# A two-layer conv-FFN backbone: another order of products in the up phase, paired accumulators, and earlier loads in the down phase

## The chip, the cores and the metric

The kernel runs on one core of a Trainium2 chip. The metric is the time of one execution in microseconds (us); runs are told by their median. The engines are TensorE (PE, with its weight loads PEld), VectorE (DVE), ScalarE (ACT), GpSimd (POOL) and SyncE (SP), on which most transfers are asked for. Each works through its own queue in order.

## What is computed

Two layers over 1024 latent tokens and 256 context tokens of width 1024. Each layer is a mixer followed by a gated FFN with a convolution of three taps along the tokens. Only the FFN with its norms, and the output projection ahead of it, matter here:

```python
def conv_ffn(h, w_up, conv_w, conv_b, w_down):
    u = dwconv(h @ w_up, conv_w, conv_b)
    return (jax.nn.silu(u[..., :D_FF]) * u[..., D_FF:]) @ w_down
...
        x = x + mods_x[2] * out_x
        x = x + mods_x[5] * conv_ffn(modulate(x, mods_x[3], mods_x[4]), ffn_w_up[layer], ffn_conv_w[layer],
                                     ffn_conv_b[layer], ffn_w_down[layer])
```

D_FF is 2816, that is 22 tiles of 128 features, each with a gate and an up half. In layer 0 the context tokens go through the same FFN; layer 1 needs the latent tokens alone.

## The kernel before, in words

Numbers are fp32. A product of full accuracy is made of three matmuls: every operand is split into a high part (a copy on ACT, L64) and a low part (a subtraction on DVE, L65), and high x high, low x high and high x low are added up in PSUM (L253 to L255). So each weight tile that comes in as wraw becomes wh (ACT) and wl (DVE) before PE can use it.

An FFN has three stages. `emit_out` makes the output projection in chunks of tokens (512, 512, and 256 of context); each result is drained from PSUM by DVE into the residual xr (L1322), and a norm follows each chunk: squares on ACT (L145), their sum on DVE (L147), a sum over partitions on PE (L151), an inverse square root by Newton steps on DVE (L71 to L81).

`emit_up` walks over the 22 features f. The first is made densely. For the others the 1024 latent tokens and the 1024 inputs are taken as 2x2 blocks b00, b01, b10, b11, and seven block products of 12 matmuls with 512 columns give what eight would (a scheme of the Strassen kind): t1, t2, t4 are sums of blocks made once per layer, and the weights' sums are made for each feature on POOL (ws, L363, L364, L367, L368) from the raw weights a (gate) and b (up) and then split into wsh and wsl. In layer 0 two products of 24 narrow matmuls for the context come on top. DVE puts the products together, ACT and DVE make the convolution from PSUM (ACT Identity L658, DVE L661 and L662), and gate times up (L386) goes to DRAM as yd (L387).

`emit_down` takes yd back in groups of features (yr, split into yh and yl), multiplies with the down weights and adds into the residual dx (L474).

Buffers hold the loops in step: there are two wraw, two wh and two wl, so the raw weight b of feature f+1 can only be asked for when that of f has been split and mixed. PSUM has six single banks (bk) and two small ones (sm). The order on each engine is made by a scheduler from the program's dependencies; each engine then waits at the head of its queue.

Of the kernel before, what the change touches and what calls it, by code (L numbers as in the profile page):

```python
# [18 lines left out]
KT = 8  # L19
# [31 lines left out]
class Blocks(Tokens):  # L51
# [16 lines left out]
def rsqrt_steps(nc, pool, out, a, shape, tag):  # L68
# [67 lines left out]
def norm_stats(g, x, chunk, pool, big, res, nm=""):  # L136
# [54 lines left out]
def norm_chunk(g, layer, which, x, h, chunk, pool, big, keep=False):  # L191
    res = []
    yield from norm_stats(g, x, chunk, pool, big, res)
    yield from norm_apply(g, layer, which, x, h, chunk, pool, big, res, keep=keep)
# [107 lines left out]

def emit_up(g, layer, h, sums, x, with_ctx, pending, close):
# [31 lines left out]
    lat = [[bank() for _ in range(2)] for _ in range(2)]
    dense(g, lat[0][0], ws[0], h, 0, 512)
    drain(pending, 9 if with_ctx else 12)
    dense(g, lat[1][0], ws[1], h, 0, 512)
    drain(pending, 9)
    for t in range(2):  # L340
        dense(g, lat[t][1], ws[t], h, 512, 512)
        drain(pending, 4)
    t2h, t2l = sums[1]
    ctx = [None, None]
    drain(pending)
    if with_ctx:
        for t in range(2):
            ctx[t] = small_ps(g)
            dense(g, ctx[t], ws[t], h, LAT, CTX + 2)
# [3 lines left out]
    with tc.tile_pool(name=f"fs{layer}", bufs=1, reuse_waits="tile") as sp, \  # L353
            tc.tile_pool(name=f"fc{layer}", bufs=1, reuse_waits="tile") as cp:
# [40 lines left out]
        gate = gate_out(0, (lat[0] + [ctx[0]])[:cut])  # L395
        up_out(0, (lat[1] + [ctx[1]])[:cut], gate)
        t1, t2, t4 = sums
        for f in range(1, NF):
# [4 lines left out]
            p1 = bank()  # L403
# [3 lines left out]
            p6 = bank()  # L407
            product(p6, s12, 1, t2)
            u2 = T([128, 512], "u")
            tt(out=u2, in0=p6, in1=s, op=ALU.add)  # L410
            c11 = bank()
            product(c11, w0, 1, h.blocks[1, 0])
            if more:
                n12 = mixes(raws, 0)
            tt(out=c11, in0=c11, in1=s, op=ALU.add)
            ctx = [None, None]
            if with_ctx:
                ctx[0] = small_ps(g)
                dense(g, ctx[0], w0, h, LAT, CTX + 2)
            p5 = bank()  # L420
# [3 lines left out]
            u4 = T([128, 512], "v")  # L424
            tt(out=u4, in0=p5, in1=u2, op=ALU.add)
            c12 = bank()
            product(c12, s34, 1, h.blocks[1, 1])
            tt(out=c12, in0=c12, in1=u4, op=ALU.add)  # L428
            gate = gate_out(f, [c11, c12, ctx[0]][:cut])
            if with_ctx:  # L430
                ctx[1] = small_ps(g)
                dense(g, ctx[1], w1, h, LAT, CTX + 2)
            p7 = bank()
            product(p7, s34, 0, b01)
            if more:
                s34 = mixes(raws, 1)
                s12 = n12
            tt(out=u2, in0=p7, in1=u2, op=ALU.add)
            c22 = T([128, 512], "s", bufs=2)
            tt(out=c22, in0=p5, in1=u2, op=ALU.add)  # L440
            c21 = bank()
            product(c21, w1, 1, t4)
            tt(out=c21, in0=c21, in1=u2, op=ALU.add)
            up_out(f, [c21, c22, ctx[1]][:cut], gate)


def emit_down(g, layer, with_ctx, after):
# [3 lines left out]
    ochunks = OUT_CH if with_ctx else OUT_CH[:2]  # L451
    pending = iter(())
    with tc.tile_pool(name=f"dx{layer}", bufs=2, reuse_waits="tile") as xp, \
            tc.tile_pool(name=f"dy{layer}", bufs=2, reuse_waits="tile") as yp:
        for c0, w, s in ochunks:
            a = min(c0, LAT)
            x = xp.tile([128, KT, 512], F32, tag="dx", name="dx")[:, :, :w]
            nc.sync.dma_start(out=x, in_=g.xm[layer][:, :, c0:c0 + w])
            for f0, m in DOWN_K:
                raw = yp.tile([128, 4, 512], F32, tag="yr", name="yr")[:, :m, :w]  # L460
                nc.sync.dma_start(out=raw, in_=g.yd[layer][f0:f0 + m, :, a:a + w].rearrange("f p n -> p f n"))
                y = [yp.tile([128, 4, 512], F32R, tag="y" + z, name="y" + z)[:, :m, :w] for z in "hl"]
                split(nc, raw, *y)
                for q in range(4):
                    wr = g.wp.tile([128, 1024], F32, tag="wraw", name="wraw")[:, :256 * m]
                    nc.sync.dma_start(out=wr.rearrange("p (f c) -> p f c", c=256), in_=g.ap["ffn_down"][layer, q, :, f0:f0 + m])
                    wt = [g.wp.tile([128, 1024], F32R, tag="w" + z, name="w" + z)[:, :256 * m] for z in "hl"]
                    split(nc, wr, *wt)
                    for dt in (2 * q, 2 * q + 1):
                        ps = g.bank.tile([128, 512], F32, tag="bk", name="bk")[:, :w]  # L470
                        o = 128 * (dt % 2)
# [2005 lines left out]
```

## Time and profile before

| | us |
|---|---|
| median of 3 runs | 3875.7 |
| lowest and highest | 3867.93, 3892.82 |
| the profiled execution | 3890.0 |
| its span | 3888.2 |
| PE busy in it | 3601.2 (93%) |
| DVE busy | 2504.6 (64%) |
| ACT, POOL busy | 1444.1, 284.2 |
| mean granted TensorE clock | 0.954 |

The numbered groups further down are rows of the profile's views. A timeline row is: start in us, length in us, engine, line, operation, out<-in, and in brackets the idle time of the engine just before and what ended it. A row of groups is: line, engine, operation, names, shapes, count | busy us in all, mean ns of one | idle before, and who ended it. A matmul row lasts longer than its share, since matmuls overlap; the distance of two starts is what one costs.

### The profile page before, as it was taken

What the parts mean: (1) busy time and instruction counts of PE and PEld (TensorE: products, weight loads), DVE (VectorE), ACT (ScalarE), POOL (GpSimd) and SP (SyncE); (2) the same over time, 40 slices, a digit from 0 to 9 for tenths busy, and PEclk for the clock granted to TensorE, in tenths of its full rate; (3) what the DMA queues carried; (4) which work ended last, traced back from release to release, by engine and by line L of the source; (5) the groups of instructions that cost most, each with busy time, mean ns of one, the idle gap of its engine ahead of it and who ended that gap; (6) DMA issues with size and microseconds to landing.
All of it is one profiled execution on the core that took longest, in us unless ns stands there. A gap on an engine that the chain in (4) does not pass through costs nothing.

```text
span 3888.2 us, 53052 instructions
## 1 busy us (share of the span) xinstructions
PE 3601.2 (93%) x20370; PEld 2912.9 (75%) x20370; DVE 2504.6 (64%) x4880; ACT 1444.1 (37%) x2664; POOL 284.2 (7%) x279
## 2 busy tenths in 40 slices
PE   6999999989989999979989989899998989999799
PEld 3778878866667888868778778767787767777577
DVE  6213566777787777765765666666466687777555
ACT  3322334511154444332333443553354443333222
POOL 0000000000002222100000000000001022222000
PEclk8999999989999999989999999987799989999899
DMA  5443556689751111234443343553454522222543
GB/s 186 127 145 118 163 176 224 201 278 304 250 166 59 71 69 68 71 139 129 159 141 119 95 132 112 170 174 106 142 191 154 172 73 74 76 71 79 174 151 111
DMA packets 349216, 546.20 MB, mean 140 GB/s; under 512 B 22490, under 2 KB 209634, under 8 KB 343972
## 3 DMA queue, kind: packets, MB, share of 16 engines
q1 hardware_dynamic: 339684, 524.99, 41.3%
q0 software_dynamic: 9280, 17.83, 1.6%
q8 instruction: 160, 2.62, 0.3%
q14 instruction: 92, 0.75, 0.1%
HBM read 405.11 MB, written 137.63 MB: 140 GB/s over the span
## 4 chain that ended last, share of the span: by engine, by line
PE 53%; DVE 12%; DMA 6%; ACT 4%; issue 4%; POOL 2%; SPq 0%; POOLq 0%; ACTq 0%; DVEq 0%
PE bk L255 9%; PE bk L254 9%; PE bk L253 9%; PE sm L253 3%; PE sm L254 3%; PE sm L255 3%; PE maS L2152 3%; DMA wraw<-in_ffn_up 1%; DVE wl L65 1%; PE hyp L1067 1%; PE maT L1269 1%; DMA wraw<-in_ffn_down 1%; PE hys L1235 1%; DVE wsl L65 1%; POOL ws L363 1%
## 5 line engine op out<-in xcount | busy, mean ns | idle before, releaser
L64 ACT ACTIVATE wh<-wraw 128x1024 fp32r<-128x1024 f32 (+1 forms) x291 | 283.5, 975 | 603.9 <-PE bk L254 400.0
L65 DVE TENSOR_TENSOR wl<-wraw,wh 128x1024 fp32r<-128x1024 f32 (+1 forms) x291 | 325.1, 1119 | 152.3 <-ACT wh L64 140.8
L253 PE MATMUL bk<-yh,wh 128*128 128x512 f32 (+1 forms) x880 | 334.8, 382 | 62.6 <-ACT yh L64 44.9
L253 PE MATMUL sm<-hh,wh 128*128 128x512 f32 x832 | 339.1, 408 | 8.5 <-ACT hh L184 4.1
L254 PE MATMUL sm<-hl,wh 128*128 128x512 f32 x832 | 334.9, 403 | 2.6 <-DVE hl L185 2.5
L255 PE MATMUL bk<-yh,wl 128*128 128x512 f32 (+1 forms) x880 | 329.3, 379 | 6.0 <-DVE wl L65 5.9
L255 PE MATMUL sm<-hh,wl 128*128 128x512 f32 x832 | 333.9, 402 | 0.3 <-DVE wl L65 0.3
L254 PE MATMUL bk<-yl,wh 128*128 128x512 f32 (+1 forms) x880 | 332.9, 379 | 0.5 <-DVE yl L65 0.5
L474 DVE SCALAR_TENSOR_TENSOR dx<-bk,modT,dx 128x512 f32<-128x512 f32 (+1 forms) x240 | 166.0, 696 | 193.7 <-PE bk L255 192.8
L253 PEld LDWEIGHTS bk<-yh,wh 128*128 128x128 f32 x880 | 170.3, 194 | 98.8 <-ACT yh L64 45.8
L255 PEld LDWEIGHTS bk<-yh,wl 128*128 128x128 f32 x880 | 168.2, 192 | 41.5 <-DVE wl L65 9.2
L253 PEld LDWEIGHTS sm<-hh,wh 128*128 128x128 f32 x832 | 159.2, 191 | 53.3 <-issue 7.2
L254 PEld LDWEIGHTS bk<-yl,wh 128*128 128x128 f32 x880 | 169.6, 193 | 34.2 <-DVE yl L65 1.9
L65 DVE TENSOR_TENSOR wsl<-ws,wsh 128x1024 fp32r<-128x1024 f32 x84 | 107.3, 1278 | 131.9 <-ACT wsh L64 131.8
L254 PEld LDWEIGHTS sm<-hl,wh 128*128 128x128 f32 x832 | 159.6, 192 | 39.4 <-DVE hl L185 4.7
L255 PEld LDWEIGHTS sm<-hh,wl 128*128 128x128 f32 x832 | 158.9, 191 | 36.7 <-issue 0.9
L64 ACT ACTIVATE wsh<-ws 128x1024 fp32r<-128x1024 f32 x84 | 89.2, 1062 | 241.4 <-POOL ws L364 223.9
L2152 PE MATMUL maS<-mak,maq 128*128 128x512 f32 (+3 forms) x480 | 150.1, 423 | 13.1 <-DMA mak<-mk 9.4
L658 ACT ACTIVATE fcg<-bk,fcb,fcw 128x512 f32<-128x512 f32 x88 | 68.1, 775 | 191.8 <-DVE bk L428 130.3
L363 POOL TENSOR_TENSOR ws<-wraw 128x512 f32<-128x512 f32 x42 | 57.6, 1372 | 979.0 <-DMA wraw<-in_ffn_up 594.8
L2152 PEld LDWEIGHTS maS<-mak,maq 128*128 128x128 f32 (+1 forms) x480 | 82.4, 198 | 60.6 <-issue 45.2
L253 PE MATMUL bk<-t2h,wsh 128*128 128x512 f32 x168 | 70.3, 419 | 36.9 <-DVE fcg L662 23.2
(658 smaller groups left out, 9250.5 us busy)
## 6 DMA issues: line engine op xcount, KB each, us to landing
wraw<-in_ffn_down SPq DMA_DIRECT2D x100, 512.0 KB, 3.7
wraw<-in_ffn_up SPq DMA_DIRECT2D x88, 512.0 KB, 3.3
mw<-in_mod_w SPq DMA_DIRECT2D x32, 1024.0 KB, 7.5
yd<-fcu SPq DMA_DIRECT2D x44, 512.0 KB, 3.5
yr<-yd SPq DMA_DIRECT2D x20, 1024.0 KB
dfw<-in_dft POOLq DMA_DIRECT2D x32, 512.0 KB, 6.7
wraw<-in_a_w SPq DMA_DIRECT2D x29, 512.0 KB, 3.3
wraw<-in_c_w SPq DMA_DIRECT2D x23, 512.0 KB, 3.5
```

The source lines that it names most:

```text
L64: nc.scalar.activation(out=hi, in_=src, func=ACTF.Copy)
L65: nc.vector.tensor_tensor(out=lo, in0=src, in1=hi.bitcast(F32), op=ALU.subtract)
L253: nc.tensor.matmul(ps, ah, bh, start=(i == 0), stop=False)
L254: nc.tensor.matmul(ps, ah, bl, start=False, stop=False)
L255: nc.tensor.matmul(ps, al, bh, start=False, stop=(i == n - 1))
L363: add(out=s[:, 0:512], in0=b[:, 0:512], in1=b[:, 512:], op=ALU.add)
L474: nc.vector.scalar_tensor_tensor(out=x[:, dt], in0=ps, scalar=mt[:, s, 40 + dt:41 + dt], in1=x[:, dt], op0=ALU.mult, op1=ALU.add)
L658: nc.scalar.activation(out=o, in_=ps[:, :n], func=ACTF.Identity, scale=cw[:, 1:2], bias=cb)
L1067: nc.tensor.matmul(out, a, b, start=(i == 0), stop=(i == len(pairs) - 1))
L1235: nc.tensor.matmul(ps, wk[:, ks], mk[:, k, ms], start=(k + i == 0), stop=(k == 3 and i == 2))
L1269: g.nc.tensor.transpose(dst, src, g.ident[:src.shape[0], :src.shape[0]])
L2152: mm(S[:, ks], l, r, start=(t == 0), stop=(t == 4))
```

## The change

- **Newton steps**: the inverse square root makes three instead of four, everywhere.
- **Norm sums**: the additions of squares in the FFN's norm (L147) run on POOL instead of DVE.
- **PSUM**: six single banks become two single ones and two pairs (pg, pu) of two neighbouring banks, 1024 columns each. `bank(g)` hands out single, lower half, upper half in turn. The convolution then goes over 1024 columns at once, without the columns at the seam.
- **Context**: 256 columns instead of 258, and one store of y instead of two.
- **Up loop**: the products stand in another order; the gate lies in one pair (G), the up half in the other (U); the convolution of the up half of f is put behind the first product of f+1. Both mixes of f+1 are made within feature f. The work buffers s, u, v, fcg, fcu are single.
- **Down**: groups of 2, 4, 4, 4, 4, 4 features instead of 4, 4, 4, 4, 4, 2; y and weights are asked for one group or one step ahead, y is split in twos, dx comes in four transfers, and the first y is asked for ahead of dx.

The core of the diff:

```diff
-    for _ in range(4):
+    for _ in range(3):
...
-            nc.vector.tensor_tensor(out=acc, in0=acc, in1=q, op=ALU.add)
+            (add or nc.vector).tensor_tensor(out=acc, in0=acc, in1=q, op=ALU.add)
...
-    g.bank = es.enter_context(g.tc.tile_pool(name="dbk", bufs=6, space=PSUM, reuse_waits="tile"))
+    g.bank = es.enter_context(g.tc.tile_pool(name="dbk", bufs=2, space=PSUM, reuse_waits="tile"))
+    g.pairs = es.enter_context(g.tc.tile_pool(name="dpr", bufs=1, space=PSUM, reuse_waits="tile"))
...
-DOWN_K = [(f, min(4, NF - f)) for f in range(0, NF, 4)]
+DOWN_K = [(0, 2)] + [(f, 4) for f in range(2, NF, 4)]
...
+def bank(g):
+
+    g.turn += 1
+    if g.turn % 3 == 0:
+        return g.bank.tile([128, 512], F32, tag="bk", name="bk")
+    if g.turn % 3 == 1:
+        g.half = pair_ps(g, "pg" if g.turn % 6 == 1 else "pu")
+        return g.half[:, 0:512]
+    return g.half[:, 512:]
...
+                act(out=d, in_=src[:, :m], func=ACTF.Identity, scale=w[:, 1:2], bias=b)
+                stt(out=d[:, 1:], in0=src[:, 0:m - 1], scalar=w[:, 0:1], in1=d[:, 1:], op0=ALU.mult, op1=ALU.add)
+                stt(out=d[:, :m - 1], in0=src[:, 1:m], scalar=w[:, 2:3], in1=d[:, :m - 1], op0=ALU.mult, op1=ALU.add)
...
             product(p1, w0, 0, h.blocks[0, 0])
-            s = T([128, 512], "s", bufs=2)
+            s = T([128, 512], "s")
             act(out=s, in_=p1, func=ACTF.Copy)
...
+            up_out(*done)
+            G = pair_ps(g, "pg")
+            product(G[:, 0:512], w0, 1, h.blocks[1, 0])
+            tt(out=G[:, 0:512], in0=G[:, 0:512], in1=s, op=ALU.add)
             if more:
                 n12 = mixes(raws, 0)
...
+            p6 = single()
+            product(p6, s12, 1, t2)
+            u2, u4 = T([128, 512], "u"), T([128, 512], "v")
+            tt(out=u2, in0=p6, in1=s, op=ALU.add)
             tt(out=u4, in0=p5, in1=u2, op=ALU.add)
...
+            if more:
+                n34 = mixes(raws, 1)
+            product(G[:, 512:], s34, 1, h.blocks[1, 1])
+            tt(out=G[:, 512:], in0=G[:, 512:], in1=u4, op=ALU.add)
+            c_u = context(w1)
+            U = pair_ps(g, "pu")
+            p7 = single()
             product(p7, s34, 0, b01)
+            tt(out=u2, in0=p7, in1=u2, op=ALU.add)
+            tt(out=U[:, 512:], in0=p5, in1=u2, op=ALU.add)
+            gate = gate_out(f, G, c_g)
...
+            product(U[:, 0:512], w1, 1, t4)
+            tt(out=U[:, 0:512], in0=U[:, 0:512], in1=u2, op=ALU.add)
+            done = (f, U, c_u, gate)
...
+            for k in range(0, KT, 2):
+                nc.sync.dma_start(out=x[:, k:k + 2], in_=g.xm[layer][:, k:k + 2, c0:c0 + w])
...
+            for q in range(0, m, 2):
+                split(nc, raw[:, q:q + 2], y[0][:, q:q + 2], y[1][:, q:q + 2])
...
+        ny = load_y(*units[0])
+        nw = load_wd(*units[0][1:], 0)
+        load_x(0)
```

The first place is DVE in layer 1's up loop. Before, from the split of the up weight (wl of 512 columns) on, with u, v, s the sums of products:

```order
L65 TENSOR_TENSOR wl<-wraw,wh 128x512
L386 TENSOR_TENSOR fcu<-fcg,fcu 128x1024
L410 TENSOR_TENSOR u<-bk,s 128x512
L415 TENSOR_TENSOR bk<-bk,s 128x512
L65 TENSOR_TENSOR wl<-wraw,wh 128x1024
L65 TENSOR_TENSOR wsl<-ws,wsh 128x1024
L425 TENSOR_TENSOR v<-bk,u 128x512
```

Now, from the same split on:

```order
L65 TENSOR_TENSOR wl<-wraw,wh 128x512
L397 SCALAR_TENSOR_TENSOR fcu<-pu,fcw,fcu 128x1023
L435 TENSOR_TENSOR pg<-pg,s 128x512
L398 SCALAR_TENSOR_TENSOR fcu<-pu,fcw,fcu 128x1023
L65 TENSOR_TENSOR wl<-wraw,wh 128x1024
L408 TENSOR_TENSOR fcu<-fcg,fcu 128x1024
L65 TENSOR_TENSOR wsl<-ws,wsh 128x1024
L446 TENSOR_TENSOR u<-bk,s 128x512
L65 TENSOR_TENSOR wsl<-ws,wsh 128x1024
L447 TENSOR_TENSOR v<-bk,u 128x512
L451 TENSOR_TENSOR pg<-pg,v 128x512
L397 SCALAR_TENSOR_TENSOR fcg<-pg,fcw,fcg 128x1023
```

The up half's convolution moved from ahead of the split to behind it, and with it the multiplication (now L408) and the gate weight's split; both splits of the mixed weights (wsl) of the next feature now stand ahead of v and of the gate's convolution.

The second place is SP where layer 1's up loop ends (yd are the last stores of y, yr its loads). Before:

```order
L387 DMA yd_83<-fcu 128x1024
L466 DMA wraw<-in_ffn_down 128x1024 x2
L458 DMA dx<-xm_81 128x8x512
L387 DMA yd_83<-fcu 128x1024
L458 DMA dx<-xm_81 128x8x512
L461 DMA yr<-yd_83 128x4x512 x4
```

Now:

```order
L409 DMA yd_83<-fcu 128x1024
L491 DMA yr<-yd_83 128x2x512
L491 DMA yr<-yd_83 128x4x512 x2
L499 DMA wraw<-in_ffn_down 128x512
L491 DMA yr<-yd_83 128x4x512
L409 DMA yd_83<-fcu 128x1024
L499 DMA wraw<-in_ffn_down 128x1024
L484 DMA dx<-xm_81 128x2x512 x6
```

The first loads of y moved ahead of the last store, and dx behind it.

The third place is PE in layer 0's down phase, where a product of 12 matmuls in the lower half of the pair pu ends and the product after next, in its upper half, begins:

```order
L257 MATMUL pu_14111<-yh_13925,wl_14067 128x512
L255 MATMUL bk_14144<-yh_13925,wh_14107 128x512
L256 MATMUL bk_14144<-yl_13926,wh_14107 128x512
L257 MATMUL bk_14144<-yh_13925,wl_14108 128x512
L255 MATMUL bk_14144<-yh_13925,wh_14107 128x512
L256 MATMUL bk_14144<-yl_13926,wh_14107 128x512
L255 MATMUL pu_14111<-yh_13925,wh_14066 128x512
```

Before, each product was a run of 12 into a bank of its own; now five matmuls of another product stand between the two halves, and the first matmul into the upper half waits for DVE's drain of the lower one.

## Rows read from the trace of the kernel before

**Rows 1.** Stretches: us, then busy us and count of each engine, clock, DMA

```profile
core 0: us, PE busy (x) PEld busy (x) DVE busy (x) ACT busy (x) POOL busy (x), PEclk, DMA share, GB/s
1190.00:1719.00 529.00, 529.00 (x2764) 450.16 (x2762) 391.65 (x595) 214.14 (x295) 102.83 (x84) 1.00 0.20 69
...
3180.00:3600.00 420.00, 395.65 (x1677) 316.50 (x1675) 307.79 (x476) 160.05 (x238) 96.76 (x76) 0.99 0.21 76
...
3751.00:3759.00 8.00, 0.38 (x1) 0.39 (x2) 3.08 (x3) 2.84 (x3) 0.00 (x0) 0.80 1.02 369
```

**Rows 2.** Groups on PE from 1190 to 1719 us (layer 0's up loop)

```profile
L255 PE MATMUL bk<-t1h,wsl 128*128 128x512 f32 x84 | 33.4, 398 | 0.0
```

**Rows 3.** Groups on DVE from 3180 to 3600 us (layer 1's up loop)

```profile
L661 DVE SCALAR_TENSOR_TENSOR fcg<-bk,fcw,fcg 128x511 f32<-128x511 f32 x40 | 29.7, 742 | 7.9 <-ACT fcg L658 7.9
...
L386 DVE TENSOR_TENSOR fcu<-fcg,fcu 128x1024 f32<-128x1024 f32 x20 | 24.4, 1220 | 0.2
```

**Rows 4.** Waits of PE from 3270 to 3600 us: us in total, times, longest

```profile
PE bk L253 <- DVE fcg L662: 22.6, 13, 2.9
```

**Rows 5.** Timelines of DVE, POOL and ACT in one feature of layer 1

```profile
3439.86 0.69 DVE L65 TENSOR_TENSOR wl<-wraw,wh 128x512 fp32r<-128x512 f32 x1
...
3449.10 1.33 DVE L65 TENSOR_TENSOR wsl<-ws,wsh 128x1024 fp32r<-128x1024 f32 x1 [5.08 <-ACT wsh L64]
3450.35 0.68 DVE L425 TENSOR_TENSOR v<-bk,u 128x512 f32<-128x512 f32 x1
...
3444.20 1.29 POOL L363 TENSOR_TENSOR ws<-wraw 128x512 f32<-128x512 f32 x1 [16.38 <-DMA wraw<-in_ffn_up]
...
3448.05 1.30 POOL L368 TENSOR_TENSOR ws<-wraw,ws 128x512 f32<-128x512 f32 x1
...
3449.38 1.06 ACT L64 ACTIVATE wsh<-ws 128x1024 fp32r<-128x1024 f32 x1 [0.26 <-POOL ws L368]
```

**Rows 6.** Timeline of PE around its longest wait in that loop

```profile
3298.13 0.39 PE L253 MATMUL bk<-b00h,wh 128*128 128x512 f32 x1
...
3300.62 0.39 PE L255 MATMUL bk<-b00h,wl 128*128 128x512 f32 x1
3303.96 0.48 PE L253 MATMUL bk<-t2h,wsh 128*128 128x512 f32 x1 [2.94 <-DVE fcg L662]
...
3307.36 0.63 PE L254 MATMUL bk<-t2l,wsh 128*128 128x512 f32 x1
```

**Rows 7.** Timelines of POOL and DVE where both work at once

```profile
3153.91 1.27 POOL L367 TENSOR_TENSOR ws<-wraw 128x512 f32<-128x512 f32 x1
3155.13 3.31 POOL L364 TENSOR_TENSOR ws<-ws,wraw 128x512 f32<-128x512 f32 x1
...
3154.26 3.06 DVE L65 TENSOR_TENSOR b01l<-xr,b01h 128x2048 fp32r<-128x2048 f32 x1 [1.44 <-ACT b01h L64]
...
1201.36 1.43 POOL L363 TENSOR_TENSOR ws<-wraw 128x512 f32<-128x512 f32 x1 [27.40 <-DMA wraw<-in_ffn_up]
...
1201.98 0.69 DVE L425 TENSOR_TENSOR v<-bk,u 128x512 f32<-128x512 f32 x1 [0.35 <-PE bk L255]
```

**Rows 8.** Groups on POOL from 3180 to 3600 us

```profile
L363 POOL TENSOR_TENSOR ws<-wraw 128x512 f32<-128x512 f32 x19 | 24.6, 1296 | 310.6 <-DMA wraw<-in_ffn_up 213.0 <-DVE wl L65 97.7
```

**Rows 9.** Timelines where the down phases begin: PE (both layers), SP, ACT

```profile
1739.45 1.22 PE L253 MATMUL bk<-yh,wh 128*128 128x512 f32 x2 [20.24 <-ACT yh L64]
...
3624.61 0.80 PE L253 MATMUL bk<-yh,wh 128*128 128x512 f32 x1 [24.70 <-ACT yh L64]
...
3607.43 0.33 SPq L387 DMA_DIRECT2D yd<-fcu  x1
...
3622.64 1.91 ACT L64 ACTIVATE yh<-yr 128x2048 fp32r<-128x2048 f32 x1 [19.32 <-DMA yr<-yd]
```

**Rows 10.** Groups on DVE from 1061 to 1137 us (layer 0's output projection)

```profile
L1322 DVE SCALAR_TENSOR_TENSOR xr<-bk,modT,xr 128x512 f32<-128x512 f32 x16 | 11.9, 746 | 4.7 <-PE bk L255 4.7
...
L147 DVE TENSOR_TENSOR nbig<-nbig 128x512 f32<-128x512 f32 x14 | 9.6, 687 | 1.7 <-ACT nbig L145 1.6
```

More of the change, by code (lines that the diff above doesn't have):

```diff
@@ L133, in norm_pads, with norm_stats @@
             g.nc.gpsimd.memset(t.bitcast(F32)[:, :, c:c + 1], 0.0)
-def norm_stats(g, x, chunk, pool, big, res, nm=""):
+def norm_stats(g, x, chunk, pool, big, res, nm="", add=None):
     nc = g.nc
@@ L188, in norm_apply, with norm_chunk @@
         yield 1
-def norm_chunk(g, layer, which, x, h, chunk, pool, big, keep=False):
+def norm_chunk(g, layer, which, x, h, chunk, pool, big, keep=False, add=None):
     res = []
-    yield from norm_stats(g, x, chunk, pool, big, res)
+    yield from norm_stats(g, x, chunk, pool, big, res, add=add)
     yield from norm_apply(g, layer, which, x, h, chunk, pool, big, res, keep=keep)
@@ L330, in product, with context @@
                      for k in range(4)])
+    def context(w):
+        if not with_ctx:
+            return None
+        ps = small_ps(g)
+        dense(g, ps, w, h, C0, CTX)
+        return ps
     raws = load(0)
@@ L334, in emit_up @@
     raws = load(1)
[L335 to L344, printed above, removed]
+    lat = [pair_ps(g, t) for t in ("pg", "pu")]
+    plan = (8, 2, 8, 8) if with_ctx else (10, 8, 8, 8)
+    for i, (c0, t) in enumerate(((0, 0), (0, 1), (512, 0), (512, 1))):
+        if i == 2 and not with_ctx:
+            drain(pending, 8)
+        dense(g, lat[t][:, c0:c0 + 512], ws[t], h, c0, 512)
+        drain(pending, plan[i])
     drain(pending)
[L346 to L349, printed above, removed]
+    ctx = [context(w) for w in ws]
     b01 = h.blocks[0, 1]
@@ L352, in emit_up @@
     close()
-    with tc.tile_pool(name=f"fs{layer}", bufs=1, reuse_waits="tile") as sp, \
-            tc.tile_pool(name=f"fc{layer}", bufs=1, reuse_waits="tile") as cp:
+    with tc.tile_pool(name=f"fs{layer}", bufs=1, reuse_waits="tile") as sp:
         T = lambda shape, tag, dt=F32, **k: sp.tile(shape, dt, tag=tag, name=tag, **k)
@@ L394, in emit_up @@
         s34 = mixes(raws, 1)
-        gate = gate_out(0, (lat[0] + [ctx[0]])[:cut])
-        up_out(0, (lat[1] + [ctx[1]])[:cut], gate)
+        gate = gate_out(0, lat[0], ctx[0])
+        done = (0, lat[1], ctx[1], gate)
         t1, t2, t4 = sums
@@ L402, in emit_up @@
                 raws = load(f + 1)
-            p1 = bank()
+            p1 = single()
             product(p1, w0, 0, h.blocks[0, 0])
-            s = T([128, 512], "s", bufs=2)
+            s = T([128, 512], "s")
             act(out=s, in_=p1, func=ACTF.Copy)
[L407 to L412, printed above, removed]
+            up_out(*done)
+            G = pair_ps(g, "pg")
+            product(G[:, 0:512], w0, 1, h.blocks[1, 0])
+            tt(out=G[:, 0:512], in0=G[:, 0:512], in1=s, op=ALU.add)
             if more:
                 n12 = mixes(raws, 0)
[L415 to L420, printed above, removed]
+            c_g = context(w0)
+            p5 = single()
             product(p5, s12, 0, t1)
@@ L451, in emit_down @@
     ochunks = OUT_CH if with_ctx else OUT_CH[:2]
+    side = {} if with_ctx else {"side": "right"}
     pending = iter(())
-    with tc.tile_pool(name=f"dx{layer}", bufs=2, reuse_waits="tile") as xp, \
-            tc.tile_pool(name=f"dy{layer}", bufs=2, reuse_waits="tile") as yp:
-        for c0, w, s in ochunks:
-            a = min(c0, LAT)
[L457 to L471, printed above, removed]
-                        mm3(nc, ps, [(wt[0][:, 256 * i + o:256 * i + o + 128], wt[1][:, 256 * i + o:256 * i + o + 128],
-                                      y[0][:, i], y[1][:, i]) for i in range(m)])
-                        nc.vector.scalar_tensor_tensor(out=x[:, dt], in0=ps, scalar=mt[:, s, 40 + dt:41 + dt], in1=x[:, dt],
-                                                       op0=ALU.mult, op1=ALU.add)
-                        drain(pending, 1)
-            drain(pending)
-            pending = after((c0, w, s), x)
@@ L2260, in emit_ffn @@
     nc, tc = g.nc, g.tc
+    nc = g.nc
     ws, bs, ss, xs_ = ExitStack(), ExitStack(), ExitStack(), ExitStack()
```

115 lines of the change are left out of this document (75 added, 40 removed).

## The prediction

> **What bounds the kernel now.** I read the stretches first, then the groups and waits of the two up loops, then the timelines around the places that the change touches. In layer 0's up loop PE is busy for all 529 us [rows 1]; 84 matmuls of one kind at four a feature [rows 2] make that 21 features of 25.2 us. Nothing is to be won there but the pad columns. In layer 1's loop PE is busy for 395.65 of 420 us [rows 1]; the gate product occurs 20 times [rows 3], so a feature takes 21.0 us, where 84 matmuls at 0.23 (twelve of them from 3298.13 on, [rows 6]) are 19.3. PE waits there for the gate's convolution on DVE, 22.6 us in 13 waits [rows 4].
>
> That wait ends a ring [rows 5]: the split of the up weight ends at 3440.55; only then is the next raw weight asked for, and POOL starts on it at 3444.20, 3.65 later; four additions end at 3449.35; ACT makes wsh in 1.06; DVE, idle for 5.08 with wsl at its head, splits, puts the products together and convolves; PE goes on; DVE comes round to the next split. So layer 1 is bound by the ring, not by PE, and a change of the order there is priced by walking round it. Outside the loops PE stands for 20.24 and 24.70 us where the down phases begin [rows 9] and is busy for 0.38 of 8 us at a chunk boundary [rows 1].
>
> **Layer 1's up loop.** I walk round the new ring, zero being the end of t4, the last product of a feature. The sum into U takes 0.7, the up weight's split 0.7: 1.5. The next raw weight is at POOL 3.65 later: 5.1. Meanwhile DVE, by its new order, waits for the up half's convolution (ACT at 1.5 to 2.7; a 1024-column reading of PSUM is not in the trace, I take 1.25, a little over the 1.06 of a copy of as many columns [rows 5]); its first half (1.27 for 1023 columns, between the 1.22 of a 1024-column product and two 0.742 [rows 3]) ends at 4.0, the sum into G at 4.6, its second half at 5.9. Then stand the gate weight's split and the multiplication, 1.2 each, both with two operands in SBUF, and POOL has been adding since 5.1.
>
> What that costs is seen where such work met before [rows 7]: DVE's b01l began at 3154.26, lasted 3.06, and ended 2.1 after POOL's addition at 3153.91 was over (3155.18); POOL's next, begun at 3155.13, ended at 3158.44, 1.12 after DVE's end (3157.32). Each waited for the other whole. DVE's v, which reads PSUM, ran in 0.69 beside POOL's addition of 1201.36 [rows 7]. The Trainium skill, page "SBUF — State Buffer", section "Who interferes with whom", says the same of an instruction on VectorE with two SBUF inputs and one on GpSimd that reads SBUF: one is shut out for the whole of the other. By the mean of layer 1's additions, 1.296 [rows 8], meeting would cost nothing and the loop would be the first rival's; by the rule it is the walk that follows. The mean is no evidence against it: DVE stood idle through POOL's work there [rows 5].
>
> So they alternate: POOL to 6.4, the split to 7.6, POOL to 8.9, the multiplication to 10.1, POOL to 11.4 and 12.7 (10.2 without). wsl of the first mix ends at 13.9, u at 14.5, wsl of the second at 15.7, v and the sum into G at 16.9, ACT at 18.3, DVE's first half at 19.6, u at 20.3. Only then may PE begin the next b00: its accumulator is the one bank that p7 left, as two single banks serve four products. Nine matmuls (2.1) and t4's twelve (2.8, held besides by the false tie of the two halves of U) end at 25.2. Without the collisions everything from wsl on comes 2.5 earlier: 22.7. The bounds are these two, and above them 26.7, if PE's two waits of some 3 us each let the clock fall: after its wait of 2.94 the matmuls last 0.63 instead of 0.39 for a while [rows 6], the lower level, 1.2 GHz, some 1.5 us lost. I take 25.2: (25.2 - 21.0) x 18 features, since the first two have their weights already, **+76** (+31 to +103).
>
> **Layer 0's up loop.** The same ring, with a whole up weight to split (1.2), 1280 columns in the multiplication (1.5) and four short convolutions of the context (0.4 each): split 2.3, POOL free to start at 5.95 but shut out by the multiplication (5.5 to 7.0); POOL to 8.3, the gate weight's split to 9.5, POOL to 13.4; wsl 14.6, context 15.4, u and v 16.6, wsl 17.8, sum 18.4, ACT 19.7, convolution 22.2, context 23.0, u 23.6, four matmuls of b00 24.6, t4 27.4. PE needs 25.2, so the ring, hidden before, would now set the pace by 2.2. Without the collisions it ends at 25.1, under PE's own. (27.4 - 25.2) x 18 = **+40** (0 to +45).
>
> **Down phases' begin.** In layer 0 the first load of y still stands behind the last store on SP, but is 512 KB instead of one of a row of large ones. The store is asked for 6.2 after t4 (sum, ACT, 2 x 1.27, 1.5), the load lands 3.65 later (the 512 KB load of [rows 5]), ACT takes 1.06, DVE's half 1.2: about 13 against 20.24, **-7** (-2 to -10). In layer 1 the first y's are loaded ahead of the last store. PE can go on after 0.7 with 24 matmuls, 5.5 us, but then the upper half of a pair wants its lower half drained, and the drain wants dx, which stands behind the last store: multiplication at 8.4 (two halves of y are split in between), store landed at 12, dx at 15.6, drain 16.4. That leaves about 10.5 of 24.70 idle, **-14** (-8 to -20). Before, the store went out at 3607.43 and y came at 3622.64 [rows 9], which is what falls away. At the chunk boundary the weights and y are asked for ahead and PE's 8 us [rows 1] shrink to about one: **-7** (-3 to -11, with layer 0's smaller ones).
>
> **Pairs elsewhere.** In the down phases 79 first matmuls into an upper half wait for DVE's drain of the lower; half of them with five matmuls, 1.15 us, between. A drain takes 0.75, as the projection's does [rows 10], and some 0.3 for the two hand-overs, so it is just covered unless DVE is in a split of 1.2: a mean of 0.13, **+10** (0 to +25). In the projections 13 such places have 0 to 8 matmuls between, five of them none, about 1.0 each, and 0.2 to 0.6 for others: +7. The norm sums that leave DVE, 0.687 each [rows 10], and a Newton step bring PE's start in the up phase forward by an estimated 8, less than the 14 sums add up to, since POOL's additions of 1.29 now shut out DVE's splits there: together **-1** (-10 to +8). Pad columns and Newton steps elsewhere, behind other work: **-2**.
>
> **The sum**: 76 + 40 - 7 - 14 - 7 + 10 - 1 - 2 = +95. The profiled execution (3890.0) lies 14.3 above the median; I add the sum to the median: 3875.7 + 95 = **3970.7**.
>
> **The rivals.**
> *No collisions.* POOL's work and DVE's splits slip past each other, as in layer 1 before [rows 5]. For it: the mean of 1.296 [rows 8]. Against: the new order has the split and the multiplication just where POOL starts. Layer 1 +31, layer 0 nothing, the rest -21: +10, **3886**.
> *PE sets the pace in both loops*, the other side. Place: the start of POOL's additions in layer 1. If the raw weight is there 3.0 after t4 instead of 5.1, without collisions, the ring is 20.6, PE's 19.3 and the short wait between p7 and b00: -0.4 x 20 = -8, layer 0 -2; the down phases -28, pairs covered, projections and rest -3: -41, **3835**. It decides from 2.1 us earlier on; for it speaks that both mixes are now asked for a feature ahead; against it that the load still waits for the split behind t4.
> *The clock falls too.* Both of PE's waits in a feature reach 2.9, and 1.5 a feature is lost: 18 x 1.5 = +27, **3998**. For it: the wait of 2.94 [rows 6]; against: shorter ones, most of the 13 [rows 4], left the stretch's clock at 0.99 [rows 1].
>
> **How the numbers follow.** Chances: forecast 0.45, with the clock 0.15, no collisions 0.24, PE sets the pace 0.16. The likeliest alone lies within 3915 and 4015 (layer 1's ring from 23.5 to 26.7, the pairs from 0 to +25). To hold eight in ten the range must take in the rival without collisions and reach to its better end: 3850 to 4015. About 1%, 39 us, is what a measurement of this kernel can tell from no change. Faster by more: 0.16, the second rival; within: 0.24, the first; slower: 0.60.
>
> **What would show it.** Right: POOL's additions in layer 1 of 2 us and more beside DVE's split and multiplication; a feature of about 25 in layer 1 and 27 in layer 0 with PE waiting for u (L456) ahead of b00; PE's gap of layer 1's down begin halved. Wrong: additions of 1.29 throughout, layer 0 at 25.2 a feature. If POOL starts well before 5 us after t4, the ring is not the one I walked.

## The result, and the profile after

The changed kernel takes 3976.3 us (median of 4 runs, 3970.7 to 3998.9) against 3880.0 of the kernel before (3867.9 to 3892.8), a ratio of 1.026 [1.021, 1.031]. 3970.7 had been forecast. The profiled execution of after took 3978.2 us, its span is 3976.4, 88.2 longer than the span before.

From the two traces, each stage between the same marks (first and last matmul of a product; starts and ends are PE's):

| stage | before | after | difference |
|---|---|---|---|
| layer 0: first b00 of the loop to the end of the last t4 | 531.4 | 571.5 | +40.1 |
| layer 0: end of t4 to where PE is done with the norm behind the down phase | 381.0 | 367.3 | -13.7 |
| layer 1: first product of mixed weights to the end of the last t4 | 440.3 | 527.2 | +86.9 |
| layer 1: end of t4 to the end | 288.3 | 260.6 | -27.7 |
| end of the mixer to the loop (output projection and first feature), layer 0 and layer 1 | 126.5, 149.6 | 123.9, 155.0 | -2.6, +5.4 |
| the two mixers | | | -11.4, +11.1 |

In layer 0 the changed kernel has seven matmuls of the projection ahead of the mixer's end; from the projection's very first matmul its stage is 127.3 against 126.5. The mixers differ by as much among kernels with the same mixer (the one of layer 0 ends between 1049 and 1064 us in the traces of this study; the one of layer 1 takes 917 to 930 us from its first matmul in the traces built on the changed kernel, 921 before), so they are left out of what follows.

The stretches of the two up loops and of layer 1's down phase, after (columns as in [rows 1], whose first two rows answer to the first two here):

```profile
core 0: us, PE busy (x) PEld busy (x) DVE busy (x) ACT busy (x) POOL busy (x), PEclk, DMA share, GB/s
1201.00:1742.00 541.00, 512.05 (x2639) 426.54 (x2637) 353.00 (x400) 180.99 (x199) 133.59 (x80) 1.00 0.17 62
3206.00:3714.00 508.00, 433.36 (x1687) 337.75 (x1688) 323.77 (x323) 154.88 (x160) 134.05 (x76) 0.92 0.20 64
3716.30:3976.40 260.10, 245.41 (x1056) 196.94 (x1056) 150.04 (x168) 66.86 (x68) 0.00 (x0) 0.99 0.49 158
```

PE is no longer busy throughout layer 0's loop: 29 of 541 us are waits. In layer 1 it waits for 74.6 of 508 us, and its clock fell from 0.99 to 0.92. POOL does as many additions as before and is busy for 134 instead of 97 us.

What PE waits for in the two loops, after (total, times, longest): layer 0 in the first row, layer 1 in the others, where before there was [rows 4].

```profile
PE pg L255 <- DVE fcg L398: 25.3, 20, 2.4
...
PE bk L255 <- DVE u L456: 38.8, 20, 2.8
PE bk L255 <- DVE u L446: 34.1, 19, 2.0
```

One feature of layer 1, after; t4 of the feature before ended at 3236.4. Compare [rows 5].

```profile
3237.02 0.68 DVE L65 TENSOR_TENSOR wl<-wraw,wh 128x512 fp32r<-128x512 f32 x1
3240.62 1.27 DVE L398 SCALAR_TENSOR_TENSOR fcu<-pu,fcw,fcu 128x1023 f32<-128x1023 f32 x1
3241.06 1.30 POOL L381 TENSOR_TENSOR ws<-wraw 128x512 f32<-128x512 f32 x1 [17.32 <-DMA wraw<-in_ffn_up]
3241.81 1.64 DVE L65 TENSOR_TENSOR wl<-wraw,wh 128x1024 fp32r<-128x1024 f32 x1
3242.31 2.28 POOL L385 TENSOR_TENSOR ws<-wraw 128x512 f32<-128x512 f32 x1
3243.37 2.31 DVE L408 TENSOR_TENSOR fcu<-fcg,fcu 128x1024 f32<-128x1024 f32 x1
3244.56 2.27 POOL L382 TENSOR_TENSOR ws<-ws,wraw 128x512 f32<-128x512 f32 x1
3246.91 1.30 POOL L386 TENSOR_TENSOR ws<-wraw,ws 128x512 f32<-128x512 f32 x1
3247.96 1.33 DVE L65 TENSOR_TENSOR wsl<-ws,wsh 128x1024 fp32r<-128x1024 f32 x1 [2.28 <-ACT wsh L64]
3249.21 0.68 DVE L446 TENSOR_TENSOR u<-bk,s 128x512 f32<-128x512 f32 x1
3251.72 0.70 DVE L451 TENSOR_TENSOR pg<-pg,v 128x512 f32<-128x512 f32 x1
3252.52 1.20 ACT L396 ACTIVATE fcg<-pg,fcb,fcw 128x1024 f32<-128x1024 f32 x1 [3.23 <-DVE pg L451]
3253.76 1.28 DVE L397 SCALAR_TENSOR_TENSOR fcg<-pg,fcw,fcg 128x1023 f32<-128x1023 f32 x1 [1.33 <-ACT fcg L396]
3254.96 0.68 DVE L456 TENSOR_TENSOR u<-bk,u 128x512 f32<-128x512 f32 x1
```

This is the ring that was walked: the split behind t4, the load, POOL's additions among DVE's split and multiplication, the splits of the mixes, u, v, ACT, convolution, and u (L456), for which PE has stood since p7 (b01). DVE's multiplication and POOL's second addition last 2.31 and 2.28; alone they last 1.22 [rows 3] and 1.30 [rows 8]. That holds for the whole loop: groups on POOL and on DVE from 3206 to 3714 us, after.

```profile
L382 POOL TENSOR_TENSOR ws<-ws,wraw 128x512 f32<-128x512 f32 x19 | 43.3, 2278 | 0.0
L385 POOL TENSOR_TENSOR ws<-wraw 128x512 f32<-128x512 f32 x19 | 43.2, 2276 | 0.0
L381 POOL TENSOR_TENSOR ws<-wraw 128x512 f32<-128x512 f32 x19 | 24.6, 1293 | 347.1 <-DMA wraw<-in_ffn_up 347.1
...
L408 DVE TENSOR_TENSOR fcu<-fcg,fcu 128x1024 f32<-128x1024 f32 x20 | 45.1, 2255 | 0.0
```

Where the down phases begin, after, PE's waits (they answer to [rows 9]; in layer 1 PE goes on 0.49 after t4 and is held twice afterwards):

```profile
1757.67 0.80 PE L255 MATMUL bk<-yh,wh 128*128 128x512 f32 x1 [12.38 <-ACT yh L64]
...
3721.99 0.50 PE L255 MATMUL pu<-yh,wh 128*128 128x512 f32 x1 [1.47 <-DVE fcu L398]
3731.86 0.80 PE L255 MATMUL pu<-yh,wh 128*128 128x512 f32 x1 [7.32 <-DVE dx L525]
```

### The profile page after: what moved, and what is told of

It reads as the page before. It is cut to its first block, busy times and chain, and to the rows that moved or that the text cites. A ratio compares the mean times of both kernels' runs of the same rounds, so it can differ in the third digit from the quotient of the medians.

```text
span 3976.4 us, 52389 instructions
## 1 busy us (share of the span) xinstructions
PE 3634.2 (91%) x20370; PEld 2922.4 (73%) x20370; DVE 2466.8 (62%) x4374; ACT 1413.8 (36%) x2513; POOL 407.2 (10%) x310
## 5 line engine op out<-in xcount | busy, mean ns | idle before, releaser
L65 DVE TENSOR_TENSOR wl<-wraw,wh 128x1024 fp32r<-128x1024 f32 (+1 forms) x291 | 342.1, 1176 | 173.2 <-ACT wh L64 157.3
L255 PE MATMUL bk<-yh,wh 128*128 128x512 f32 (+1 forms) x294 | 111.1, 378 | 17.6 <-ACT yh L64 12.4
L462 DVE TENSOR_TENSOR pu<-pu,u 128x512 f32<-128x512 f32 x42 | 29.4, 700 | 155.9 <-PE pu L257 155.9
L255 PE MATMUL pu<-yh,wh 128*128 128x512 f32 (+1 forms) x292 | 110.4, 378 | 14.0 <-DVE dx L525 11.9
L525 DVE SCALAR_TENSOR_TENSOR dx<-pu,modT,dx 128x512 f32<-128x512 f32 (+1 forms) x80 | 55.7, 696 | 99.2 <-PE pu L257 91.6
L257 PE MATMUL bk<-yh,wl 128*128 128x512 f32 (+1 forms) x294 | 111.0, 377 | 5.9 <-DVE wl L65 5.9
L255 PE MATMUL bk<-b00h,wh 128*128 128x512 f32 x168 | 73.6, 438 | 44.1 <-DVE u L456 43.6
L255 PE MATMUL pg<-yh,wh 128*128 128x512 f32 (+1 forms) x294 | 111.2, 378 | 0.5 <-DVE dx L525 0.5
L257 PE MATMUL pu<-yh,wl 128*128 128x512 f32 (+1 forms) x292 | 109.2, 374 | 1.1 <-DVE wl L65 1.1
L257 PE MATMUL pg<-yh,wl 128*128 128x512 f32 (+1 forms) x294 | 110.0, 374 | 0.2 <-DVE wl L65 0.2
```

What stands on the lines that cost most here:

```text
L65: nc.vector.tensor_tensor(out=lo, in0=src, in1=hi.bitcast(F32), op=ALU.subtract)
L255: nc.tensor.matmul(ps, ah, bh, start=(i == 0), stop=False)
L257: nc.tensor.matmul(ps, al, bh, start=False, stop=(i == n - 1))
L462: tt(out=U[:, 0:512], in0=U[:, 0:512], in1=u2, op=ALU.add)
L525: nc.vector.scalar_tensor_tensor(out=x[:, dt], in0=ps, scalar=mt[:, s, 40 + dt:41 + dt], in1=x[:, dt], op0=ALU.mult, op1=ALU.add)
```

## The experiments

All were timed beside the kernel before on the same chip. "A feature" is the mean distance from t4's first matmul to the next feature's, without the last one, which mixes no weights for another.

| kernel | median us | ratio to before | feature, layer 0 | feature, layer 1 |
|---|---|---|---|---|
| before | 3879 to 3884 | 1 | 25.30 | 21.0 |
| after | 3976.3 | 1.026 [1.021, 1.031] | 27.09 | 25.35 |
| old loops, new down phase | 3838.1 | 0.989 [0.986, 0.991] | 25.30 | 21.1 |
| third raw buffer | 3910.8 | 1.008 [1.005, 1.010] | 27.08 | 21.8 |
| no meetings | 3919.4 | 1.011 [1.008, 1.013] | 25.5 | 24.1 |
| filled wait | 3968.3 | 1.023 [1.020, 1.027] | 27.09 | 24.4 |
| no meetings, filled wait | 3885.5 | 1.002 [1.000, 1.004] | 25.4 | 22.5 |
| u first | 3945.1 | 1.016 [1.014, 1.019] | 27.09 | 23.7 |
| third raw buffer, u first | 3885.0 | 1.001 [0.999, 1.002] | 27.10 | 20.50 |
| old loops, new down, third raw buffer | 3798.3 | 0.979 [0.977, 0.982] | 25.30 | 19.37 |
| norm sums on DVE | 3974.7 | 1.024 [1.022, 1.026] | 27.10 | 25.2 |

**The new down phase alone.** Kernel before, with the whole `emit_down` of after and its groups, on the six single banks:

```diff
-                    ps = bank(g)[:, :w]
+                    ps = g.bank.tile([128, 512], F32, tag="bk", name="bk")[:, :w]
```

> The kernel before, with the new down phase alone (groups of 2, 4, 4, 4, 4, 4, early y and weights, dx in four transfers), into the six single banks as before. Theory (the down phases are a separate account, and what their traces show of the changed kernel, 13.7 less in layer 0 and 27.7 less in layer 1, is owed to the loads alone): up loops as before at 25.3 and about 21.0 us a feature, down phases 41 shorter, 3839 in all. By the prediction's own terms without the pairs (-7 -14 -7): 28 shorter, 3852. Rival (the pairs gave part of the gain, or the early loads need the new up loop's end): the down phases within 10 of before, 3870 to 3880.

Measured: 40.6 less than before, as the theory had it, and 13 more than the prediction's terms without the pairs. By stages (end of t4 on): layer 0 367.9, as after with its pairs; layer 1 254.4, 6.2 less than after. So with the pairs layer 0's down phase is no longer. In layer 1 the kernels part at the begin, where six banks let PE run on until dx is there:

```profile
3582.66 2.07 PE L253 MATMUL bk<-yh,wh 128*128 128x512 f32 x4 [3.54 <-ACT yh L64]
3586.21 0.80 PE L254 MATMUL bk<-yl,wh 128*128 128x512 f32 x1 [1.48 <-DVE yl L65]
...
3600.96 0.50 PE L255 MATMUL bk<-yh,wl 128*128 128x512 f32 x1 [1.07 <-DVE wl L65]
```

These waits together are 6.1, where after has 9.3 with the 7.32 for dx. The two kernels also end their up loops differently, so the 6.2 is not shown to be the price of the pairs alone.

**The head of the ring: a third buffer.** Kernel after; g.raws, the number of raw buffers, is 3 in layer 1 alone (the same edit stands at every wraw):

```diff
-            raw = g.wp.tile([128, 1024], F32, tag="wraw", name="wraw")
+            raw = g.wp.tile([128, 1024], F32, tag="wraw", name="wraw", bufs=g.raws)
...
-    open_weights(g, ws)
+    open_weights(g, ws, 2 if with_ctx else 3)
```

> The changed kernel with three instead of two buffers for raw weights in layer 1 alone (layer 0 is the control). The order of products, of sums and of matmuls stays. Theory (the ring: split of the up weight behind t4, load, POOL): the load no longer waits for the split behind t4, POOL starts long before wsl wants it, and what is left a feature is 84 matmuls (19.3) and the wait for u (L456) behind L397, about 1.2: 20.6; layer 1's loop 527 to about 433, 3882 in all, layer 0 as it was at 27.1. Rival (the two single banks and two pairs are what holds PE: b00 waits for the bank of p7 whatever POOL does): 24 to 25 a feature, 3965 to 3976.

Measured: 65 less than after, layer 0 as it was. The ring is broken: of PE's two waits the one for u (L446) ahead of p7 is gone, 30.4 us in 19 waits for the other u remain. The size was missed by 29: the fastest features take 20.9 and have the wait of 1.29 that was expected (1.2), but others take up to 23.1. The third buffer does not only take the load out of the ring: POOL's additions come earlier, the multiplication and the gate weight's split are back at 1.22, and POOL now meets the splits of the mixes (1.45 in the mean for 1.27). PE in a longer and in a shorter feature (u's line is L457 in this kernel):

```profile
3402.45 0.47 PE L256 MATMUL bk<-b00h,wh 128*128 128x512 f32 x1 [1.98 <-DVE u L457]
...
3403.97 0.63 PE L257 MATMUL bk<-b00l,wh 128*128 128x512 f32 x1
...
3425.00 0.47 PE L256 MATMUL bk<-b00h,wh 128*128 128x512 f32 x1 [1.29 <-DVE u L457]
...
3426.00 0.39 PE L257 MATMUL bk<-b00l,wh 128*128 128x512 f32 x1
```

Behind the wait of 1.98 the matmuls last 0.63 and stand 0.43 apart, the clock's lower level (1.2 GHz); behind that of 1.29 they do not.

**The meetings.** Kernel after, with one operand of each colliding instruction of DVE in PSUM:

```diff
-            tt(out=o, in0=gate, in1=o, op=ALU.mult)
+            tt(out=o[:, 0:LAT], in0=gate[:, 0:LAT], in1=pair, op=ALU.mult)
+            if with_ctx:
+                tt(out=o[:, LAT:], in0=gate[:, LAT:], in1=o[:, LAT:], op=ALU.mult)
...
-                w0 = halves(raws[0])
+                w0 = halves(raws[0], other=U0)
...
+            act(out=t[0], in_=raw, func=ACTF.Copy)
+            stt(out=t[1], in0=other, scalar=0.0, in1=raw, op0=ALU.mult, op1=ALU.add)
```

> The changed kernel with the two colliding instructions of DVE taking one of their two operands from PSUM: the multiplication multiplies the gate with the unconvolved up half in the pair, and the gate weight's low part is the raw weight plus zero times that pair. So the result of the up phase is another one; every instruction, wait and transfer else is there. Theory (meeting of DVE's and POOL's work costs the ring 2.5 us): POOL's additions 1.29 throughout, the multiplication 1.25; layer 1 from a mean of 25.1 to 22.7 a feature (-50), layer 0 from 27.1 to PE's own 25.2 (-38): 3888. Rival (the additions are longer, but off the ring, or PE's waits take it up): 3960 to 3976.

Measured: the additions last 1.30 throughout, beside the multiplication's 1.22 (groups on POOL and on DVE from 3206 to 3640 us):

```profile
L386 POOL TENSOR_TENSOR ws<-ws,wraw 128x512 f32<-128x512 f32 x18 | 23.4, 1300 | 0.0
...
L412 DVE TENSOR_TENSOR fcu<-fcg,pu 128x1024 f32<-128x1024 f32 x18 | 22.0, 1221 | 0.6
```

The gate weight's low part no longer needs ACT's high part either, but in the kernel after DVE never stood for that in layer 1's loop. Layer 0 falls to 25.5, nearly the 25.2 that were expected. Layer 1 falls only to 24.1 instead of 22.7, with this wait in each feature:

```profile
PE bk L255 <- DVE u L463: 53.1, 19, 3.1
```

These are 2.8 each, and behind each the nine matmuls of b00 stand 0.40 apart in the mean instead of 0.23, 1.5 us lost. The next two runs ask whether that is the clock or a link that the walk did not see.

**The wait filled.** Kernel after, in layer 1:

```diff
             product(p7, s34, 0, b01)
+            if not with_ctx:
+                spare = small_ps(g)
+                mm3(nc, spare, [(s34[0][:, 128 * k:128 * k + 128], s34[1][:, 128 * k:128 * k + 128], b01[0][:, k], b01[1][:, k])
+                                for k in range(2)])
```

> The changed kernel with six matmuls more per feature in layer 1, of b01 with the mixed weights into a spare bank that nobody reads, put into PE's wait ahead of b00: 1.4 us of the 2.8 are filled. Theory (features of 24.45 are the ring at full clock; the 25.1 to 27.3 of others are the clock's falls after a wait of 2.8): with waits of 1.4 no b00 after the wait lies at 0.44 instead of 0.23, every feature takes 24.4 to 24.5, the loop is 14 shorter: about 3962. Rival (the ring itself is longer in these features, by a later load or a longer addition): the features stay as they are, and the six matmuls cost nothing or add up to 1 each: 3976 to 3995.

Measured: six matmuls of no use make a feature 0.9 shorter, 24.4, what the quick features of after take. Loop after (upper row) and filled, each from t4 to t4 over 20 features:

```profile
3209.00:3711.00 502.00, 428.43 (x1672) 333.69 (x1670) 319.98 (x318) 152.36 (x159) 134.05 (x76) 0.93 0.21 65
...
3208.00:3693.00 485.00, 430.91 (x1794) 338.85 (x1792) 322.58 (x318) 153.08 (x159) 133.98 (x76) 0.98 0.21 67
```

PE is busy for 2.5 us more with 122 more matmuls recorded, the clock is 0.98 instead of 0.93, and the loop is 17 shorter. The median is 8 less (runs from 3958.3 to 3976.7, which takes in the 3962 that were expected); the runs of the two kernels overlap, so it is the loop that decides between theory and rival.

**Both.**

> The kernel without meetings of DVE and POOL (the multiplication and the gate weight's low part as in the run of that name, so the up phase has another result), and with the six spare matmuls in PE's wait ahead of b00. That kernel took 23.9 a feature in layer 1, where 22.7 was expected; each of its features shows a wait of 2.78 and nine matmuls of b00 at 0.41 behind it. Theory (the ring without meetings is 22.6, and what is over that is the clock alone): 22.4 to 22.7 a feature, 19.37 + waits, about 26 less than 3919: 3893. Rival (the ring has another link of 1.3 that the walk did not see): 23.9, 3919.

Measured: 22.5 a feature and 3885.5, 34 less than without the filling. The loop, t4 to t4, without meetings and then with the wait filled too:

```profile
3171.00:3650.00 479.00, 423.11 (x1674) 332.56 (x1672) 291.76 (x318) 152.46 (x159) 96.95 (x76) 0.93 0.19 68
...
3169.00:3617.00 448.00, 421.35 (x1791) 333.06 (x1790) 292.12 (x318) 152.62 (x159) 96.99 (x76) 1.00 0.21 73
```

So the ring without meetings is 22.5, the meetings cost 24.4 - 22.5 = 1.9 at full clock, and what was missing in the run before was the clock.

**The tail of the ring: u ahead of the convolution.** Kernel after, two raw buffers, layer 1, an order on DVE alone:

```diff
+                    tc.add_manual_dep(i.ins, first.ins.name, mybir.DependencyInfo(mybir.DependencyClass.NoSync, mybir.DependencyReason.DATA), reason="order")
```

where `i` is the convolution's first half (L397) of the gate and `first` is u2 = p7 + u2 (L456).

> The changed kernel with two raw-weight buffers, and the same move on DVE in layer 1: u2 ahead of the gate's convolution. Theory (ACT and the first half of the convolution are a link of the ring, since b00 waits for the bank that u2 frees and t4 follows it): the ring loses the time from p7's end to u2's start, 1.9 us: 24.45 becomes 22.6, with less or no fall of the clock the mean goes from 25.1 to 22.6 to 23.1, 3925 to 3935. Rival (the ring closes through t4's other input, U's upper half or the false tie of its two halves, so b00's start is not what counts): 24.5 to 25.1, 3965 to 3976.

Measured: features of 22.5 to 22.7 and of 23.9 to 24.3, 23.7 in the mean; 31 less than after, where 41 to 51 were expected. The wait ahead of b00 is down to 0.88, as it must be if b00 only waits for the bank. The other one remains:

```profile
PE bk L255 <- DVE u L448: 35.2, 19, 2.0
PE bk L255 <- DVE u L458: 16.6, 19, 0.9
```

The rival falls: b00's start does count. The 22.5 is the ring less 1.9. In 13 of the 19 features p7's matmuls behind the first wait (1.7 to 2.0) stand 0.43 apart for a while; the wait ahead of b00 is 0.88 in all of them and so can't take that up, and it costs.

**Both ends.**

> The changed kernel with three raw-weight buffers in layer 1 (as in the run of that name) and, on DVE in layer 1, the sum u2 = p7 + u2 put ahead of the first half of the gate's convolution; nothing else moves but the sum into U's upper half, which goes one place up with it. Theory (with the third buffer what is left is the bank of p7, which u2 frees only behind ACT and the convolution; the waits of 1.98 to 2.03 there let the clock fall, those of 1.29 do not): PE waits 0.85 ahead of b00, no fall, 20.3 a feature instead of the mean of 21.75: 3882. Rival (the clock falls and the longer features of that run come from POOL's meetings with the splits of the mixes, which stay): 21.5 to 21.8, 3905 to 3911.

Measured: every feature 20.50, one wait of 0.87 in each (besides one of 2.7 ahead of the last t4, PE's waits come down to 16.6 us in 19), and the clock stays up:

```profile
3202.00:3612.00 410.00, 390.73 (x1674) 312.44 (x1673) 299.42 (x319) 152.38 (x158) 108.25 (x73) 1.00 0.23 79
```

Without the waits of 2 us there is no fall, though POOL still meets DVE in this kernel (108.25 us busy against 97). At 3885.0 it is level with the kernel before, 91 less than after by one buffer and one place in a queue.

**The old loop with a third buffer.** The kernel before, the new down phase, three raw buffers in layer 1.

> The kernel before with the new down phase, and three raw-weight buffers in layer 1. Theory (layer 1's loop was bound by the same ring of split, load and POOL before the change, at 21.0 to 21.3 a feature, and PE's own pace is the 19.37 of its first four features): the loop falls to 19.4 to 19.8 a feature, 30 to 35 less than the 3838 of the same kernel with two buffers: 3805. Rival (the waits of PE for the gate's convolution come from the banks or from DVE's order, whatever the load does): 21.0 to 21.3, 3838.

Measured: 19.37 in every feature, PE busy without a gap:

```profile
3143.00:3531.00 388.00, 388.00 (x1684) 315.86 (x1684) 328.52 (x482) 164.04 (x239) 96.92 (x76) 1.00 0.24 83
```

The loop before hung on the same ring. This kernel is the fastest of the study, 2.1% below before and 4.5% below after.

**Norm sums.** Kernel after without `add=nc.gpsimd`.

> The changed kernel with the FFN's sums of squares back on DVE. The stage from the start of the output projection to the loop's first t1 took 125.8 (layer 0) and 155.0 (layer 1) in the changed kernel. By the prediction's term (the move brings PE's start forward by about 8, less POOL's meetings with DVE's splits; -10 to +8 in both): the two stages together 0 to 8 longer, 3976 to 3984. Rival (POOL's additions shut out DVE's splits there and are longer themselves, which is why layer 1's stage became 5.4 longer than before): layer 1's stage back at 150, layer 0's within 2: 3970.

Measured: 3974.7, no difference; the stages from the mixer's end to the first t1 are 124.6 and 153.6 against 125.9 and 155.0. Neither the term nor the rival shows. Layer 1's projection itself, after and with the sums on DVE, is 6 to 7 longer than the 98.3 of before in both cases:

```profile
3033.50:3138.90 105.40, 98.13 (x401) 74.79 (x402) 58.28 (x80) 43.57 (x62) 20.80 (x13) 0.97 0.50 168
...
3028.10:3132.50 104.40, 97.59 (x403) 74.87 (x404) 60.75 (x93) 43.98 (x62) 0.00 (x0) 0.98 0.51 170
```

## Why the prediction was right, and where not

**Right in its mechanism.** The ring of split, load, POOL, splits, sums, ACT and convolution sets the pace of layer 1, and now of layer 0. Taking out its head, its middle or its tail shortened it in three separate runs, and with head and tail gone PE has the one wait that the bank of p7 leaves. No run has the old order with the pairs or the new order with six banks, so what the order costs and what the fewer banks cost was not separated. The rival in which PE sets the pace failed where it was said to: POOL starts 4.7 after t4, not 3.0. The rival without meetings failed by the 2.28 and 2.31. The Trainium skill, page "SBUF — State Buffer", section "Who interferes with whom", says that a VectorE instruction with two SBUF inputs contends with a GpSimd instruction that reads SBUF, and that the port pair which the two engines share is an exclusive lock. The trace agrees, down to which operand counts: with one of them in PSUM the multiplication took 1.22 beside POOL's 1.30.

**Layer 1's loop, +76, measured +86.9: two misses that cancelled and one that did not.** (1) The walk came out at 25.2, the ring at full clock is 24.4: POOL started at 4.7 and not at 5.1, as the load took 3.4 for 3.65, and POOL's four additions were stretched from 5.2 to 7.15 (3241.06 to 3248.21 above), not to 7.6, since each engine went on about 1.1 after the other's end instead of a whole 1.2 to 1.3. The two kernels with the filled wait give the same 1.9 for the meetings. (2) The clock's fall was kept for the rival at 1.5 a feature, 15 in 100; it costs 0.9 in the mean, for it falls in some features only (next section). So 25.2 was met by 24.4 + 0.9 = 25.3, a ring shorter than the forecast's with a fall of the clock that the forecast's branch left out: that the two meet is luck. (3) The ring was taken to bind 18 features. It binds from the first on: 24.5 from the first t4 to the second, where before had 19.37 for its first four, and only the last feature is free of it. At 21 features the term would have been 88.

**Layer 0's loop, +40, measured +40.1.** 27.09 a feature for 27.4, and 25.30 before for 25.2: 1.8 a feature instead of 2.2, or 34 over 19 features. The other 6 come ahead of the first t4, which the prediction did not count, so that the term is right to 0.1 is luck. PE's long wait is for the second half of the gate's convolution (L398) ahead of b10, and not, as the prediction said, for u (L456) ahead of b00; that one is 0.3. Without meetings the ring goes back under PE's pace (25.4 and 25.5 a feature), and the stage takes 539.1 instead of 571.5: the meetings are 32 of the 40.

**The down phases' begin, -7 and -14, measured -7.9 and -15.4.** In layer 0 the terms as written add up to 12.1, not to 13, and 12.4 was measured: the load came 5.1 after the store was asked for instead of 3.65, and PE began without DVE's half of 1.2. In layer 1 the multiplication ended 7.9 after t4 (8.4 forecast) and the drain of the first lower half 16.0 after it (16.4).

**Boundary and pairs in the down phases, -7 + 10 = +3, measured -18.** This term was the furthest off. The pairs' +10 was sized at a mean of 0.13 in 79 places; behind the begins PE waits for the drain of a pair in five places, 4.2 us in layer 0 and 0.8 in layer 1, and the kernel with single banks has layer 0's down phase no shorter. The boundary's -7 was right for the 8 us in [rows 1] but left out what a stall costs behind it: with 25 and 8 us of stalls PE was busy for 251.2 us from 3624.6 on before, for the same 1056 matmuls that take 245.4 after (shown above).

```profile
3624.60:3888.20 263.60, 251.16 (x1056) 200.03 (x1056) 147.51 (x154) 63.80 (x57) 0.00 (x0) 0.98 0.42 132
```

The first matmul behind the stall lasted 0.80 [rows 9]. That this is the clock alone was not separated; the granted mean went from 0.98 to 0.99.

**Projections and norms, -1, measured +2.8.** The projections did get longer, but mostly not by the pairs' mechanism: layer 1's is 7.1 longer (98.3 to 105.4), layer 0's some 4, and the waits that grew in layer 1 are those for wh on ACT (0.7 us in 2 waits before, 4.8 in 6 after), with PE now at work on two weights at once; only in layer 0 are there 3.4 us in 3 waits for the drain of a lower half. What was gained lies behind it: PE's wait for the context's norm fell from 15.1 to 4.0. With the sums on DVE that wait is 10.1, but the stage is no longer: with the sums on POOL the waits ahead of that norm come to 16.2 instead of 11.1, and PE is busy for 102.1 instead of 99.0 us in the stage. What the missing Newton step is worth by itself was not tried.

**The sum**, +95 for +88 between the traces and +96 between the medians, is better than its terms, and that is luck: the +11 too little in layer 1 and the +21 too much in the down phases offset each other.

## What to carry to other kernels

Where an engine waits once per loop turn, walk the ring back to the buffer at its head before reordering what lies on it: one more buffer (4 KB a partition) was worth 40 us in the old order and 65 in the new one. When work moves to the time at which POOL adds, look which DVE instructions there read two operands from SBUF; here one operand in PSUM was enough to be out of the way. And an instruction that frees the only bank for the next product stands best ahead of a long one that nobody waits for.

## What the runs showed of the hardware

**PE's clock falls behind some waits of under 3 us.** In layer 1's loops up to the last t4, in the ten traces that have such waits (before, after and eight experiments), none of 126 waits of 0.5 to 1.71 us is followed within nine matmuls by three or more that stand some 0.43 apart (the lower level, 1.2 GHz); of 88 waits of 1.73 to 2.1 us 48 are, and of 40 from 2.5 to 3.3 all but three. What parts the waits of one length from each other stays open. Whether a fall costs is a matter of what stands behind it. In the feature shown above the clock fell in p7, behind a wait of 1.76; the ring had slack there, the wait behind p7 shrank from 2.8 to 1.22, and nothing was lost. In the next one the fall came behind 2.77, in b00, where it costs:

```profile
3249.94 0.50 PE L255 MATMUL bk<-b01h,wsh 128*128 128x512 f32 x1 [1.76 <-DVE u L446]
...
3250.84 0.63 PE L255 MATMUL bk<-b01h,wsh 128*128 128x512 f32 x1
...
3255.78 0.47 PE L255 MATMUL bk<-b00h,wh 128*128 128x512 f32 x1 [1.22 <-DVE u L456]
...
3280.15 0.47 PE L255 MATMUL bk<-b00h,wh 128*128 128x512 f32 x1 [2.77 <-DVE u L456]
...
3281.83 0.63 PE L255 MATMUL bk<-b00h,wh 128*128 128x512 f32 x1
```

A matmul of no use in such a wait can therefore shorten a loop: 17 us by six a feature in one kernel, 31 between the two stretches of the kernels without meetings.

**A tiny instruction pays for a whole meeting.** In the kernel before, while POOL adds, Newton steps of two columns on DVE last eight times as long as the one ahead of POOL's first addition:

```profile
1166.70 0.15 DVE L77 TENSOR_TENSOR nw2t<-nr 128x2 f32<-128x2 f32 x1
...
1170.24 1.19 DVE L81 SCALAR_TENSOR_TENSOR nr<-nw2t,nr 128x2 f32<-128x2 f32 x1
...
1171.37 1.25 POOL L364 TENSOR_TENSOR ws<-ws,wraw 128x512 f32<-128x512 f32 x1
1171.46 1.19 DVE L77 TENSOR_TENSOR nw2t<-nr 128x2 f32<-128x2 f32 x1
```
